# Softmax probabilities scaled in two steps, and latent norms behind each token tile's latent projection, in a two-layer hybrid-attention decoder

## The chip, the cores and the metric

The kernel runs on one core of one Trainium2 chip. The metric is the device time of one execution in microseconds (us). A core has a matrix engine (TensorE, PE in the rows, with PEld for its weight loads), a vector engine (VectorE, DVE), an activation engine (ScalarE, ACT), a general engine (GpSimd, POOL) and a queue engine that issues most of the transfers (SyncE, SP). Each engine executes its own list of instructions strictly in order, and waits on the others through semaphores.

## The reference

Two decoder layers over 512 tokens of width 1024, all in float32. Each layer has four groups of four attention heads, 64 wide, that share one input and one output projection, and then a SwiGLU network. The latent part of the third group (MLA), whose norms the change touches, and the attention that all groups end in are:

```python
h = rmsnorm(x, g_pre_mix[l])
z = jnp.einsum('bsd,de->bse', h, w_in[l])
z_moba, z_fox, z_fg, z_cq, z_ckv, z_kr, z_dil = jnp.split(z, SPLIT_POINTS, axis=-1)
...
c_q = rmsnorm(z_cq, g_mla_q[l])          # 192 wide
q_c = to_heads(jnp.einsum('bsr,re->bse', c_q, w_mla_q_up[l]), N_HEADS_MLA)
c_kv = rmsnorm(z_ckv, g_mla_kv[l])       # 128 wide
kv = to_heads(jnp.einsum('bsr,re->bse', c_kv, w_mla_kv_up[l]), N_HEADS_MLA)
...
sc = jnp.where(key_pos[None, :] <= q_pos[:, None], sc, -jnp.inf)   # every group: its own mask
p = jax.nn.softmax(sc, axis=-1)
return jnp.einsum('bhqk,bhkd->bhqd', p.astype(v.dtype), v)
...
x = x + rmsnorm(y, g_post_mix[l])        # y: output projection of the four groups
```

## The kernel before, in words

Tokens lie in four tiles of 128. Every float32 product is made of three matmuls on split operands (`mm3`: high by high, high by low, low by high), so each weight chunk is fetched into one of five `wraw` buffers by SyncE, copied to its high part by ScalarE (L168) and subtracted to its low part by VectorE (L173) or GpSimd (L171).

**A layer's first half (`mixing`).** The values of the first group (called fox) are projected, and token tile by token tile the latents: `ps_lat` (24 matmuls) is copied to `lat[t]` by ScalarE (L551). The fox queries follow (`ps_qk`, 24 matmuls for two heads). In a later loop over the token tiles the kernel before normalises the latents: ScalarE squares and sums (L595, L596), GpSimd makes the inverse root (L598 to L600), VectorE multiplies by it and by the gains `gqkv` (L601 for the 192 query columns, L602 for the 128 key-value columns); then TensorE turns the tile (transposes into `cq0T`, `cq1T`, `ckvT`, L604 to L606). The turned latents are split (`split`, L610 and L611, and `q1_stk`, L616 and L617), which is what the projections `ps_qup` and `ps_kvup` read.

**Attention (`attend`).** A unit is one head and a range of query tiles: four tiles (24 units: fox, MLA and MoBA heads in both layers) or two (16 units: the dilated heads). Per query tile TensorE makes scores `ps_s` (L454), VectorE adds the mask and finds the row's bound (`neg`, L457), and ScalarE takes the exponential with its row sum (L459, into `pr` and `den`). Query tile 0 has 128 keys, tile 3 has 512. After the last of them VectorE takes one reciprocal of all sums (L462), and GpSimd multiplies each tile of `pr` by it (L465). Then TensorE transposes blocks of 128x128 out of `pr` into `pT` (L474), ScalarE and VectorE split them (`turn`, L476 and L477), and TensorE applies them to the values (`weigh`, into `ps_o`, L482 and L483). The first turn of a four-tile unit takes the key tile 0 of all four query tiles. `weave` writes the units down so that the next unit's scores stand ahead of this unit's transposes, with projection matmuls of other groups in between; its two `pr` buffers allow that.

The order on each engine is that of the program as written, as a list scheduler rearranges it: it takes the instruction that stands earliest in the program among those that it estimates to be ready, and buffers of the pools (two `pr`, two banks for scores, two for transposes) hold it back. So moving a few lines also moves what stands around them, on every engine.

Of the kernel before, what the change touches and what calls it, by code (L numbers as in the profile page):

```python
# [9 lines left out]
F32 = mybir.dt.float32  # L10
F32R = mybir.dt.float32r
I32 = mybir.dt.int32
AF = mybir.ActivationFunctionType
ALU = mybir.AluOpType
PSUM = bass.MemoryType.PSUM

P = 128
# [6 lines left out]
EPS = 1e-6  # L24
# [13 lines left out]
L_CQ, L_CKV, L_KR = 4, 196, 324  # L38
# [43 lines left out]
def decoder(ctx, tc, x, positions, w_in, b_forget, g_mla_q, w_mla_q_up, g_mla_kv, w_mla_kv_up,  # L82
            w_out, g_pre_mix, g_post_mix, w_gate, w_up, w_down, g_pre_ffn, g_post_ffn, consts, out):
    nc = tc.nc
# [4 lines left out]
    small = ctx.enter_context(tc.tile_pool(name="small", bufs=8))  # L89
# [11 lines left out]
    def R(dt, name):  # L101
        return keep.tile([P, 512], dt, name=name, tag="ring", bufs=NR)

    def T(dt, name):
        return keep.tile([P, 512], dt, name=name, tag="temp", bufs=NTMP)
# [24 lines left out]
    mhalf = keep.tile([P, 2], F32, name="mhalf")  # L130
# [143 lines left out]
    def mixing(l, h_in, in_slots, out_slots, w_first):  # L274
# [163 lines left out]
        def attend(e0, tag, h, qa, qb, passes, vt, bias, more):  # L438
# [8 lines left out]
            for qt in range(qa, qb):  # L447
# [11 lines left out]
                nc.scalar.activation(p, p, AF.Exp, bias=neg[:, qt:qt + 1], scale=-1.0, accum_out=den[:, qt - qa:qt - qa + 1])  # L459
                offs[qt] = off  # L460
                off += nk
            nc.vector.reciprocal(den, den)  # L462
            for qt in range(qa, qb):
                p = pr[:, offs[qt]:offs[qt] + (qt + 1) * P]
                nc.gpsimd.tensor_scalar(p, p, den[:, qt - qa:qt - qa + 1], 1.0, op0=ALU.mult, op1=ALU.mult)  # L465
            yield
            ncol = (qb - qa) * P
            po = bank(ps_o, "ps_o")
# [63 lines left out]
        def window(col):  # L532
# [8 lines left out]
        lat_lo = [slot(s, F32R, "lat_lo") for s in out_slots[1:3]]  # L541
        wl = [weights(w_in[l, k * P:(k + 1) * P, C_LAT:C_LAT + N_LAT], [N_LAT],
                      into=(lat_hi[:, k, :], lat_lo[k // 4][:, k % 4, 0:N_LAT])) for k in range(KD)]
        for t in range(NT):
            for _ in steps[t][1]():
                pass
            ps = bank(ps_mm, "ps_lat")
            ts = slice(t * P, (t + 1) * P)
            for k in range(KD):
                mm3(ps[:, 0:N_LAT], hh(k, ts), hl(k, ts), *wl[k], k == 0, k == KD - 1)  # L550
            nc.scalar.copy(lat[t][:, 0:N_LAT], ps[:, 0:N_LAT])  # L551

        fox_passes, fox_qk = proj_qk(C_FOX, False)
        run(fox_qk[:1])
# [27 lines left out]
        if l == 0:  # L582
            with tc.issue_after(normed[0].ins), tc.issue_after(normed[1].ins):
                rope_tables()
        gains_lat = R(F32, "gqkv")
        gq, gkv = gains_lat[:, 0:192], gains_lat[:, 192:320]
        nc.sync.dma_start(gq, g_mla_q[l:l + 1, :].broadcast_to([P, 192]))
        nc.sync.dma_start(gkv, g_mla_kv[l:l + 1, :].broadcast_to([P, P]))
        jk = T(F32, "jk")
        pq0, pq1 = bank(ps_t, "cq0T"), bank(ps_t, "cq1T")  # L590
        pkv = bank(ps_s, "ckvT")
        for t in range(NT):
            ss = small.tile([P, 2], F32, name="ss2", tag="ss2")
            zq, zkv = lat[t][:, L_CQ:L_CKV], lat[t][:, L_CKV:L_KR]
            nc.scalar.activation(jk[:, 0:192], zq, AF.Square, accum_out=ss[:, 0:1])  # L595
            nc.scalar.activation(jk[:, 192:320], zkv, AF.Square, accum_out=ss[:, 1:2])  # L596
            r = small.tile([P, 2], F32, name="r2", tag="r2")
            nc.gpsimd.tensor_scalar(r[:, 0:1], ss[:, 0:1], 1.0 / 192, EPS, op0=ALU.mult, op1=ALU.add)  # L598
            nc.gpsimd.tensor_scalar(r[:, 1:2], ss[:, 1:2], 1.0 / 128, EPS, op0=ALU.mult, op1=ALU.add)
            nc.gpsimd.tensor_tensor(r, r, mhalf, op=ALU.pow)  # L600
            nc.vector.scalar_tensor_tensor(zq, zq, r[:, 0:1], gq, op0=ALU.mult, op1=ALU.mult)  # L601
            nc.vector.scalar_tensor_tensor(zkv, zkv, r[:, 1:2], gkv, op0=ALU.mult, op1=ALU.mult)  # L602
            ts = slice(t * P, (t + 1) * P)
            nc.tensor.transpose(pq0[:, ts], lat[t][:, L_CQ:L_CQ + P], ident)  # L604
            nc.tensor.transpose(pq1[0:64, ts], lat[t][:, L_CQ + P:L_CKV], ident)
            nc.tensor.transpose(pkv[:, ts], zkv, ident)  # L606
# [445 lines left out]
```

## Time and profile before

| what | value |
|---|---|
| time, median of 3 runs | 1266.09 us (1265.72 to 1267.85) |
| the profiled execution | 1268.2 us; span in the profile 1266.4 us |
| granted TensorE clock, mean | 0.996 of full speed |
| TensorE matmul busy | 1228.6 us, 97% of the span, 7044 matmuls |
| VectorE, ScalarE, GpSimd busy | 821.4 us (65%), 646.4 us (51%), 225.5 us (18%) |
| first halves of the two layers | about 14 to 265 us and 652 to 895 us of the span |

The span is what the profiler sees of the execution; 1.8 us of the time lie around it. A matmul's end is modelled in the records, so that matmuls that follow each other closely seem to overlap; the distance from start to start is what one takes.

### The profile page before, as it was taken

The page shows a single profiled execution, that of the slowest core. Times are in us where ns is not written, and L with a number is a line of the kernel's source. Part 1 is how long each engine was busy: PE and PEld are TensorE (multiplying, and loading weights), DVE is VectorE, ACT ScalarE, POOL GpSimd, SP SyncE. Part 2 cuts the span into 40 slices and gives each one's busy share as a digit, 9 for nine tenths or more (in the row PEclk, how much of TensorE's full clock was granted, in tenths as well). Part 3 has the DMA queues.
Part 4 walks back from the last instruction along what each step waited for, and adds up shares of the span by engine and source line. Part 5 has one row for each costly group of instructions (what it writes and reads, how often), then busy time and mean ns, then how long its engine had stood idle before and what let it go on. Part 6 is the DMA issues. An engine that isn't in the chain of part 4 may idle for free.

```text
span 1266.4 us, 19777 instructions
## 1 busy us (share of the span) xinstructions
PE 1228.6 (97%) x7044; PEld 1063.4 (84%) x7044; DVE 821.4 (65%) x1621; ACT 646.4 (51%) x1403; POOL 225.5 (18%) x305
## 2 busy tenths in 40 slices
PE   8999999999999999999999999999899999999998
PEld 7878877779989898888788788778798989898886
DVE  6876866787766666533466668676787666674334
ACT  6676756754434344422456767667553434353332
POOL 3223334443000000000131324433430000000001
PEclk9999999989999999999999999999999999999999
DMA  7221241521433333433342222324224333334331
GB/s 230 72 60 42 66 116 55 172 68 34 127 99 107 93 109 92 125 100 100 125 117 73 59 56 70 100 88 137 68 64 126 95 108 97 105 100 123 94 93 75
DMA packets 158054, 121.60 MB, mean 96 GB/s; under 512 B 9090, under 2 KB 133122, under 8 KB 157956
## 3 DMA queue, kind: packets, MB, share of 16 engines
q1 hardware_dynamic: 151908, 111.55, 30.3%
q10 hardware_dynamic: 6048, 8.80, 2.6%
q8 instruction: 55, 0.90, 0.3%
q14 instruction: 43, 0.35, 0.1%
HBM read 111.93 MB, written 4.19 MB: 92 GB/s over the span
## 4 chain that ended last, share of the span: by engine, by line
PE 75%; DVE 4%; ACT 2%; POOL 2%; issue 2%; DMA 1%; DVEq 0%; POOLq 0%; ACTq 0%; SPq 0%
PE ps_g L198 6%; PE ps_g L197 6%; PE ps_g L199 6%; PE ps_d L197 6%; PE ps_d L199 6%; PE ps_d L198 6%; PE ps L197 5%; PE ps L199 5%; PE ps L198 5%; PE ps_s L454 2%; PE ps_out L199 2%; PE pT L474 2%; PE ps_out L198 2%; PE ps_out L197 2%; PE ps_qk L197 2%; PE ps_qk L198 2%
## 5 line engine op out<-in xcount | busy, mean ns | idle before, releaser
L173 DVE TENSOR_TENSOR wlo<-wraw,whi 128x512 fp32r<-128x512 f32 x249 | 179.9, 729 | 149.7 <-ACT whi L168 144.8
L168 ACT CAST whi<-wraw 128x512 fp32r<-128x512 f32 x268 | 163.9, 620 | 213.2 <-PE ps_d L199 121.0
L198 PE MATMUL ps_g<-h,whi 128*128 128x512 f32 (+1 forms) x384 | 144.2, 376 | 5.0 <-DVE h L231 5.0
L197 PE MATMUL ps_g<-h,whi 128*128 128x512 f32 (+1 forms) x384 | 143.9, 375 | 1.4 <-ACT h L231 1.2
L199 PE MATMUL ps_g<-h,wlo 128*128 128x512 f32 (+1 forms) x384 | 143.6, 374 | 0.0
L876 ACT CAST whi<-wsum 128x512 fp32r<-128x512 f32 x80 | 49.7, 622 | 149.4 <-PE ps_g L198 71.9
L240 POOL TENSOR_SCALAR rstd<-ssp 128x1 f32<-128x1 f32 x16 | 6.9, 433 | 647.8 <-ACT jk L236 647.7
L465 POOL TENSOR_SCALAR pr<-pr,den 128x128 f32<-128x128 f32 (+3 forms) x128 | 78.1, 629 | 192.1 <-DVE den L462 188.6
L197 PE MATMUL ps_d<-whi,fh 128*128 128x512 f32 x288 | 112.2, 390 | 0.0
L199 PE MATMUL ps_d<-whi,fl 128*128 128x512 f32 x288 | 112.1, 389 | 0.0
L198 PE MATMUL ps_d<-wlo,fh 128*128 128x512 f32 x288 | 112.0, 389 | 0.0
L877 DVE TENSOR_TENSOR wlo<-wsum,whi 128x512 fp32r<-128x512 f32 x80 | 54.9, 690 | 83.0 <-ACT whi L876 83.0
L197 PE MATMUL ps<-sum,whi 128*128 128x256 f32 x320 | 90.2, 282 | 0.0
L198 PE MATMUL ps<-sum,whi 128*128 128x256 f32 x320 | 90.1, 282 | 0.0
L199 PE MATMUL ps<-sum,wlo 128*128 128x256 f32 x320 | 90.1, 281 | 0.0
L198 PEld LDWEIGHTS ps_g<-h,whi 128*128 128x128 f32 x384 | 73.1, 190 | 18.0 <-DVE h L231 6.2
L197 PEld LDWEIGHTS ps_g<-h,whi 128*128 128x128 f32 x384 | 73.1, 190 | 14.5 <-ACT h L231 2.7
L199 PEld LDWEIGHTS ps_g<-h,wlo 128*128 128x128 f32 x384 | 73.2, 191 | 12.6
L197 PE MATMUL ps_qk<-h,whi 128*128 128x512 f32 x192 | 76.8, 400 | 0.0
L199 PE MATMUL ps_qk<-h,wlo 128*128 128x512 f32 x192 | 75.7, 394 | 0.0
L198 PE MATMUL ps_qk<-h,whi 128*128 128x512 f32 x192 | 75.7, 394 | 0.0
L459 ACT ACTIVATE pr<-pr,neg 128x128 f32<-128x128 f32 (+3 forms) x128 | 71.5, 560 | 5.9 <-DVE neg L457 4.9
(312 smaller groups left out, 3335.2 us busy)
## 6 DMA issues: line engine op xcount, KB each, us to landing
wraw<-in_w_gate_dram SPq DMA_DIRECT2D x88, 256.0 KB, 3.4
wraw<-in_w_up_dram SPq DMA_DIRECT2D x88, 256.0 KB, 3.1
wraw<-in_w_down_dram SPq DMA_DIRECT2D x88, 256.0 KB, 2.8
wraw<-in_w_in_dram SPq DMA_DIRECT2D x72, 256.0 KB, 3.0
wraw<-in_w_out_dram SPq DMA_DIRECT2D x32, 256.0 KB, 2.9
xt<-in_x_dram SPq DMA_DIRECT2D x16, 256.0 KB, 4.4
rope_b<-rope_a ACTq DMA_DIRECT2D x64, 64.0 KB, 2.0
wraw<-in_w_in_dram SPq DMA_DIRECT2D x16, 178.0 KB, 3.6
```

The lines of the kernel that those rows point to most:

```text
L168: nc.scalar.copy(hi, raw)
L173: nc.vector.tensor_tensor(lo, raw, f32(hi), op=ALU.subtract)
L197: nc.tensor.matmul(ps, a_hi, b_hi, start=start, stop=False)
L198: nc.tensor.matmul(ps, a_hi, b_lo, start=False, stop=False)
L199: last_mm[0] = nc.tensor.matmul(ps, a_lo, b_hi, start=False, stop=stop)
L240: nc.gpsimd.tensor_scalar(r, ss[:, 0:1], ss[:, 1:2], EPS, op0=ALU.add, op1=ALU.add)
L454: nc.tensor.matmul(ps[:, 0:w], a if a.shape[-1] == P else a[:, qt * P:(qt + 1) * P], b[:, 0:w], start=i == 0, stop=i == n - 1)
L459: nc.scalar.activation(p, p, AF.Exp, bias=neg[:, qt:qt + 1], scale=-1.0, accum_out=den[:, qt - qa:qt - qa + 1])
L465: nc.gpsimd.tensor_scalar(p, p, den[:, qt - qa:qt - qa + 1], 1.0, op0=ALU.mult, op1=ALU.mult)
L474: nc.tensor.transpose(pt[:, i * P:(i + 1) * P], pr[:, offs[qt] + kt * P:offs[qt] + (kt + 1) * P], ident)
L876: nc.scalar.copy(hi, raw)
L877: nc.vector.tensor_tensor(lo, raw, f32(hi), op=ALU.subtract)
```

## The change

Two things. In `attend`, the reciprocal and the scaling of all query tiles but the last are written directly behind the last but one tile's exponential, as one reciprocal of three sums (of one sum in a two-tile unit) and a scaling per tile; the last tile has a reciprocal of its own and its scaling. The scalings are the same 128 in the whole program; there are 80 reciprocals instead of 40. In `mixing`, the squares, the inverse root and the two multiplications of a token tile's latents are written directly behind that tile's latent projection, and the transfers of their gains (`gqkv`) directly behind those of the latent weights. The matmuls are the same 7044.

```diff
                 nc.scalar.activation(p, p, AF.Exp, bias=neg[:, qt:qt + 1], scale=-1.0, accum_out=den[:, qt - qa:qt - qa + 1])
                 offs[qt] = off
                 off += nk
-            nc.vector.reciprocal(den, den)
-            for qt in range(qa, qb):
-                p = pr[:, offs[qt]:offs[qt] + (qt + 1) * P]
-                nc.gpsimd.tensor_scalar(p, p, den[:, qt - qa:qt - qa + 1], 1.0, op0=ALU.mult, op1=ALU.mult)
+
+                if qt >= qb - 2:
+                    new = range(qa, qt + 1) if qt == qb - 2 else [qt]
+                    d = den[:, new[0] - qa:qt - qa + 1]
+                    nc.vector.reciprocal(d, d)
+                    for t in new:
+                        p = pr[:, offs[t]:offs[t] + (t + 1) * P]
+                        nc.gpsimd.tensor_scalar(p, p, den[:, t - qa:t - qa + 1], 1.0, op0=ALU.mult, op1=ALU.mult)
             yield
...
                       into=(lat_hi[:, k, :], lat_lo[k // 4][:, k % 4, 0:N_LAT])) for k in range(KD)]
+        gains_lat = R(F32, "gqkv")
+        gq, gkv = gains_lat[:, 0:192], gains_lat[:, 192:320]
+        nc.sync.dma_start(gq, g_mla_q[l:l + 1, :].broadcast_to([P, 192]))
+        nc.sync.dma_start(gkv, g_mla_kv[l:l + 1, :].broadcast_to([P, P]))
+        jk = T(F32, "jk")
         for t in range(NT):
...
             nc.scalar.copy(lat[t][:, 0:N_LAT], ps[:, 0:N_LAT])
+            ss = small.tile([P, 2], F32, name="ss2", tag="ss2")
+            zq, zkv = lat[t][:, L_CQ:L_CKV], lat[t][:, L_CKV:L_KR]
+            nc.scalar.activation(jk[:, 0:192], zq, AF.Square, accum_out=ss[:, 0:1])
+            nc.scalar.activation(jk[:, 192:320], zkv, AF.Square, accum_out=ss[:, 1:2])
+            r = small.tile([P, 2], F32, name="r2", tag="r2")
+            nc.gpsimd.tensor_scalar(r[:, 0:1], ss[:, 0:1], 1.0 / 192, EPS, op0=ALU.mult, op1=ALU.add)
+            nc.gpsimd.tensor_scalar(r[:, 1:2], ss[:, 1:2], 1.0 / 128, EPS, op0=ALU.mult, op1=ALU.add)
+            nc.gpsimd.tensor_tensor(r, r, mhalf, op=ALU.pow)
+            nc.vector.scalar_tensor_tensor(zq, zq, r[:, 0:1], gq, op0=ALU.mult, op1=ALU.mult)
+            nc.vector.scalar_tensor_tensor(zkv, zkv, r[:, 1:2], gkv, op0=ALU.mult, op1=ALU.mult)
```

The same lines are gone from the later loop, which keeps its transposes.

What this does to the order of the engines is seen at three places. First TensorE at the latents of the first layer; it is the same in the second. `ps_qk` are the fox queries and, behind them, the fox keys; the three transposes per token tile write `cq0T`, `cq1T` and `ckvT`. Before, from the last matmuls of the keys on:

```order
L198 MATMUL ps_qk<-h,whi 128x512
L199 MATMUL ps_qk<-h,wlo 128x512
L604 MATMUL cq0T<-cst,lat 128x128
L605 MATMUL cq1T<-cst,lat 64x128
L604 MATMUL cq0T<-cst,lat 128x128
L605 MATMUL cq1T<-cst,lat 64x128
L606 MATMUL ckvT<-cst,lat 128x128
L197 MATMUL ps_qk<-h,whi 128x512
L606 MATMUL ckvT<-cst,lat 128x128
L198 MATMUL ps_qk<-h,whi 128x512
L604 MATMUL cq0T<-cst,lat 128x128
```

With the change, from the last matmuls of the queries on:

```order
L198 MATMUL ps_qk<-h,whi 128x512
L199 MATMUL ps_qk<-h,wlo 128x512
L609 MATMUL cq0T<-cst,lat 128x128
L610 MATMUL cq1T<-cst,lat 64x128
L611 MATMUL ckvT<-cst,lat 128x128
L609 MATMUL cq0T<-cst,lat 128x128
L610 MATMUL cq1T<-cst,lat 64x128
L611 MATMUL ckvT<-cst,lat 128x128
L609 MATMUL cq0T<-cst,lat 128x128
L610 MATMUL cq1T<-cst,lat 64x128
L611 MATMUL ckvT<-cst,lat 128x128
```

The twelve transposes stood behind 45 of the 48 `ps_qk` matmuls and among the last three; now they stand together behind the first 24, and the other 24 come between them and the first `ps_qup`.

Second, VectorE at the first MoBA head of the first layer (buffers numbered, since two units are in flight; `den` are this unit's sums, `v`, `wearly` and `wlo` other work, `mixf` the output of the unit before). Before:

```order
L457 ISA neg_1830 128x1
L477 TENSOR_TENSOR ptb1_96<-pT_1899,ptb0_95 128x384
L309 TENSOR_TENSOR v_889<-ps_v_1874,v_889 128x2x128
L173 TENSOR_TENSOR wearly_2270<-wraw_2276,wearly_2270 128x512
L462 RECIPROCAL den_1831<-den_1831 128x4
L173 TENSOR_TENSOR wlo_2053<-wraw_2051,whi_2052 128x512
L173 TENSOR_TENSOR wlo_2059<-wraw_2057,whi_2058 128x512
L173 TENSOR_TENSOR wlo_2116<-wraw_2114,whi_2115 128x512
L522 TENSOR_TENSOR mixf_1826<-ps_o_1858,mixt_1827 64x512
```

With the change:

```order
L457 ISA neg_1838 128x1
L481 TENSOR_TENSOR ptb1_96<-pT_1908,ptb0_95 128x384
L466 RECIPROCAL den_1839<-den_1839 128x3
L309 TENSOR_TENSOR v_889<-ps_v_1883,v_889 128x2x128
L173 TENSOR_TENSOR wearly_2282<-wraw_2288,wearly_2282 128x512
L466 RECIPROCAL den_1839<-den_1839 128x1
L173 TENSOR_TENSOR wlo_2063<-wraw_2061,whi_2062 128x512
L173 TENSOR_TENSOR wlo_2069<-wraw_2067,whi_2068 128x512
L457 ISA pr_1955,neg_1953<-ps_s_1956,cst_79 128x128
```

The reciprocal of three sums stands two instructions further ahead than the one of four stood, and that of the last sum stands in the old place.

Third, SyncE in the second layer, where the gains' two transfers lie among those of the weights (`128x356` are the latent weights, `x_mid` the first layer's output). Before:

```order
L167 DMA wraw<-in_w_in_dram 128x356 x4
L167 DMA wraw<-in_w_in_dram 128x4x128
L1020 DMA x_mid_78<-xt 128x512 x2
L167 DMA wraw<-in_w_in_dram 128x4x128 x3
L167 DMA wraw<-in_w_mla_q_up_dram 128x384
L182 DMA wraw<-in_w_mla_q_up_dram 64x384 x2
L167 DMA wraw<-in_w_mla_kv_up_dram 128x512
L167 DMA wraw<-in_w_in_dram 128x4x128 x4
L167 DMA wraw<-in_w_in_dram 128x2x256 x2
L587 DMA gqkv<-in_g_mla_q_dram 128x192
L588 DMA gqkv<-in_g_mla_kv_dram 128x128
L167 DMA wraw<-in_w_in_dram 128x2x256 x2
```

With the change:

```order
L167 DMA wraw<-in_w_in_dram 128x356 x4
L550 DMA gqkv<-in_g_mla_q_dram 128x192
L551 DMA gqkv<-in_g_mla_kv_dram 128x128
L167 DMA wraw<-in_w_in_dram 128x4x128
L1025 DMA x_mid_78<-xt 128x512 x2
```

The two transfers moved ahead of the 14 other weight transfers that stood in front of them. In the first layer they stand behind the third of the eight latent weight chunks.

## Rows read from the trace of the kernel before

**Rows 1.** The page: busy time of each engine with its share of the span and its instructions.

```profile
PE 1228.6 (97%) x7044; PEld 1063.4 (84%) x7044; DVE 821.4 (65%) x1621; ACT 646.4 (51%) x1403; POOL 225.5 (18%) x305
```

**Rows 2.** The waits of the whole span: engine, tile and line that waited, what released it; us in total, times, longest. PE are waits of the matmul stream, PEld those of the weight loads ahead of it.

```profile
PE pT L474 <- POOL pr L465: 7.2, 15, 0.9
...
PEld pT L474 <- POOL pr L465: 16.7, 35, 1.3
...
POOL pr L465 <- DVE den L462: 188.6, 29, 24.7
...
DVE den L462 <- ACT pr L459: 8.7, 14, 1.0
...
PE ps_lat L198 <- DVE lat_lo L173: 0.3, 1, 0.3
```

**Rows 3.** The timeline of the second layer's first fox head: start in us, duration, engine, line, instruction with how many of it in a row; in brackets the idle time ahead of it and what ended it.

```profile
700.26 0.72 ACT L459 ACTIVATE pr<-pr,neg 128x512 f32<-128x512 f32 x1
...
701.22 0.17 DVE L462 RECIPROCAL den<-den 128x4 f32<-128x4 f32 x1
...
701.49 3.18 POOL L465 TENSOR_SCALAR pr<-pr,den 128x128 f32<-128x128 f32 x4 [24.71 <-DVE den L462]
...
702.66 0.65 PE L474 MATMUL pT<-cst,pr 128*128 128x128 f32 x2
...
703.55 0.33 PE L474 MATMUL pT<-cst,pr 128*128 128x128 f32 x1 [0.24 <-POOL pr L465]
...
704.72 0.66 PE L474 MATMUL pT<-cst,pr 128*128 128x128 f32 x4 [0.84 <-POOL pr L465]
```

**Rows 4.** The timeline of the first layer's first MoBA head, from its last exponential to its first transposes, in the same columns.

```profile
154.31 0.71 ACT L459 ACTIVATE pr<-pr,neg 128x512 f32<-128x512 f32 x1
...
155.41 0.17 DVE L462 RECIPROCAL den<-den 128x4 f32<-128x4 f32 x1
155.65 1.99 DVE L173 TENSOR_TENSOR wlo<-wraw,whi 128x512 fp32r<-128x512 f32 x3
...
155.75 3.46 POOL L465 TENSOR_SCALAR pr<-pr,den 128x128 f32<-128x128 f32 x4 [8.92 <-DVE den L462]
...
157.16 0.33 PE L474 MATMUL pT<-cst,pr 128*128 128x128 f32 x1
...
159.27 0.66 PE L474 MATMUL pT<-cst,pr 128*128 128x128 f32 x4 [0.34 <-POOL pr L465]
```

**Rows 5.** TensorE's timeline at other units that stop: the third fox head, the third MoBA head (x5 in 1.42 us) and the first dilated head, all of the first layer.

```profile
95.32 0.66 PE L474 MATMUL pT<-cst,pr 128*128 128x128 f32 x4 [0.34 <-POOL pr L465]
...
191.52 1.42 PE L474 MATMUL pT<-cst,pr 128*128 128x128 f32 x5
...
210.39 0.55 PE L474 MATMUL pT<-cst,pr 128*128 128x128 f32 x3 [0.87 <-POOL pr L465]
```

**Rows 6.** Durations: four scalings in a row with no such instruction of VectorE beside them (timeline), and the reciprocals by form (busy us, mean ns of one, idle ahead of them).

```profile
122.84 2.06 POOL L465 TENSOR_SCALAR pr<-pr,den 128x128 f32<-128x128 f32 x4 [5.49 <-DVE den L462]
...
L462 DVE RECIPROCAL den<-den 128x4 f32<-128x4 f32 x24 | 4.2, 176 | 6.1 <-ACT pr L459 5.6
...
L462 DVE RECIPROCAL den<-den 128x2 f32<-128x2 f32 x16 | 2.6, 162 | 3.1 <-ACT pr L459 3.1
```

**Rows 7.** The latents: the multiplications by form, then the timeline of the second layer in order of time (GpSimd's last inverse root, the gains' first transfer, VectorE's first multiplications, TensorE's `ps_qk`, transposes, `ps_cum` and projections, the first splits).

```profile
L601 DVE SCALAR_TENSOR_TENSOR lat<-lat,r,gqkv 128x192 f32<-128x192 f32 x8 | 3.1, 411 | 2.5 <-DMA gqkv<-in_g_mla_q_dram 2.5
L602 DVE SCALAR_TENSOR_TENSOR lat<-lat,r,gqkv 128x128 f32<-128x128 f32 x8 | 2.6, 345 | 0.0
...
673.78 0.69 POOL L600 TENSOR_TENSOR r<-r,mhalf 128x2 f32<-128x2 f32 x1
...
679.20 0.46 SPq L587 DMA_DIRECT2D gqkv<-in_g_mla_q_dram  x1
...
681.70 0.39 PE L198 MATMUL ps_qk<-h,whi 128*128 128x512 f32 x1
681.93 0.39 PE L199 MATMUL ps_qk<-h,wlo 128*128 128x512 f32 x1
...
682.28 0.75 DVE L601 SCALAR_TENSOR_TENSOR lat<-lat,r,gqkv 128x192 f32<-128x192 f32 x2 [0.73 <-DMA gqkv<-in_g_mla_q_dram]
...
682.75 0.33 PE L604 MATMUL cq0T<-cst,lat 128*128 128x128 f32 x1 [0.44 <-DVE lat L601]
...
684.98 0.27 PE L606 MATMUL ckvT<-cst,lat 128*128 128x128 f32 x1
685.09 0.29 PE L679 MATMUL ps_cum<-fg,cst 128*128 128x16 f32 x2
...
685.90 0.42 PE L197 MATMUL ps_qup<-whi,sp_hi 128*128 128x384 f32 x1
...
686.17 0.68 DVE L611 TENSOR_TENSOR sp_lo<-cq0T,sp_hi 128x512 fp32r<-128x512 f32 x1
...
687.19 0.40 PE L198 MATMUL ps_kvup<-wlo,sp_hi 128*128 128x512 f32 x1
```

**Rows 8.** Windows of 2 us where a layer's first half hands over to its network, two of the first layer and one of the second: length, busy time of each engine with its instructions, then the granted TensorE clock, the DMA share and GB/s.

```profile
278.00:280.00 2.00, 1.27 (x6) 0.97 (x5) 2.00 (x3) 0.92 (x3) 0.43 (x1) 0.50 0.40 117
...
282.00:284.00 2.00, 2.00 (x11) 2.00 (x11) 2.00 (x4) 0.40 (x1) 0.00 (x0) 0.50 0.00 0
...
907.00:909.00 2.00, 2.00 (x17) 2.00 (x18) 1.35 (x3) 0.73 (x2) 0.86 (x2) 1.00 0.00 0
```

More of the change, by code (lines that the diff above doesn't have):

```diff
@@ L584, in mixing @@
                 rope_tables()
[L585 to L589, printed above, removed]
         pq0, pq1 = bank(ps_t, "cq0T"), bank(ps_t, "cq1T")
@@ L592, in mixing @@
         for t in range(NT):
[L593 to L602, printed above, removed]
+            zkv = lat[t][:, L_CKV:L_KR]
             ts = slice(t * P, (t + 1) * P)
```

## The prediction

> **What bounds the kernel now.** I read the page first: TensorE is busy 97% of the span [rows 1], so a change that leaves its 7044 matmuls as they are can only gain where TensorE stands still, and can only lose by making it stand still more. Next the table of waits, for what TensorE stands still for. In the layers' first halves the largest entry is the transposes' wait for GpSimd's scalings: 7.2 us in 15 stops of the matmul stream, and 16.7 us in 35 stops of the weight loads, part of which the matmul ahead covers [rows 2]. GpSimd in its turn waits for VectorE's reciprocal, and that for the exponentials, 8.7 us in 14 times (0.62 each) [rows 2]. Third, the timelines at those stops. In the second layer's first fox head the last exponential begins at 700.26 and takes 0.72; one reciprocal at 701.22; four scalings of 3.18 us together from 701.49; and TensorE, which came to the transposes at 702.66, gets the third block at 703.55 and the last four at 704.72 [rows 3]. The first three scalings needed nothing of the last exponential: that is the latency that the change attacks. The other stop is at the latents: the multiplication waits 0.73 us for gains that SyncE issued at 679.20, and the transposes wait for it [rows 7].
>
> What a stop costs is more than its gap. From 703.55 to 704.72 are 1.17 us; less the gap of 0.84 and one transpose of 0.11 (684.98 to 685.09 [rows 7]) 0.22 is left for starting up again [rows 3].
>
> **The scalings.** By starts minus 0.11 for each transpose, the units lose: first fox head 1.8 us (702.66 to 704.72 is 2.06, less three pitches of 0.11 is 1.73 [rows 3]); first MoBA head 2.0 (157.16 to 159.27 is 2.11, less 0.33 is 1.78, and the start-up of its last stop [rows 4]); third MoBA head 0.9 (five in 1.42 instead of 0.55 [rows 5]); first dilated head 1.1 (0.87 + 0.22); third fox head 0.6 (0.34 + 0.22) [rows 5]. With some 1.0 for the other dilated heads that is 7.4 us per layer, 14.8 in the two: between the 7.2 and the 16.7 of the two kinds of waits, as it must be, since 7.2 + 15 x 0.22 = 10.5 leaves out the stops that show only as stretched groups of transposes.
>
> What comes back is less. In the MoBA head the third exponential is over when the last begins, at 154.31, and the reciprocal now stands at 155.41 [rows 4]; with the change its first reciprocal stands two instructions further ahead on VectorE, right behind the exponential, so the scalings begin some 0.9 us earlier; in the fox head 1.0 (end of the third exponential near 700.3, against 701.22). The last tile's scaling takes its turn behind those three, so the last block is ready by about as much earlier, not by the whole wait. And the scheduler, which sees the scalings earlier, also moves transposes ahead: by the matmuls between a unit's last score and its transposes (0.11 to 0.23 each), the first fox head's first three stand 1.4 us earlier and its fourth 0.7, the third MoBA head's first 0.7, and the second layer's first halves nearly the same; only the first MoBA head's fourth stands 0.8 later, with the next unit's scores in the gap. So I leave waits of 1.2 us in each first fox head, 0.6 in each first and each third MoBA head, 0.6 in each first dilated head, 0.1 in each third fox head and 0.4 per layer in the rest: 3.5 per layer, 7.0 in all. **Gain 14.8 - 7.0 = 7.8 us.**
>
> Whether GpSimd can use its earlier start hangs on who works beside it. Four scalings take 2.06 us alone [rows 6], but 3.46 where three of VectorE's weight subtractions, each with two inputs in SBUF, run in the same stretch, and these take 1.99, 0.66 each [rows 4]. So GpSimd slows and VectorE doesn't. The earlier scalings meet the same subtractions and one more, at some 0.4 us for each; this is in the 0.6 left for the MoBA heads. The Trainium skill ("SBUF — State Buffer", section "Who interferes with whom") says that such a VectorE instruction and a GpSimd instruction that reads SBUF contend for one port pair, that whoever issues first holds it and the other blocks fully. By that rule an earlier GpSimd would hold VectorE up instead, up to a whole scaling at a time; the trace agrees that they contend but shows GpSimd paying (3.46 against 2.06).
>
> **The latents.** TensorE's last `ps_qk` ahead of the transposes starts at 681.93; with a pitch of 0.23 (681.70 to 681.93) its successor could start at 682.16, and starts at 682.75. From 681.93 to 685.09 stand four `ps_qk` and twelve transposes, 4 x 0.23 + 12 x 0.11 = 2.24; it takes 3.16, so 0.92 are lost. Then 685.90 to 687.19, three matmuls of some 0.18 and one of 0.23, 0.77, take 1.29: 0.52 lost to the splits [rows 7]. With 0.1 behind that it is 1.5 us, and by the same count 1.7 in the first layer. With the change the last token tile's inverse root is done at 673.78 + 0.69 = 674.47, and two multiplications of 0.41 and 0.35 make 675.2; the transposes stand 21 matmuls earlier, 682.16 - 21 x 0.23 = 677.3. So 2.1 us are spare. Behind them 24 matmuls of 0.23, 5.5 us, now lie ahead of the first `ps_qup`; the splits, three casts and three subtractions of 0.68 that partly overlap [rows 7], need some 4. **Gain 3.2 us**, and if VectorE should have a queue there, 1.6.
>
> The eight pairs of multiplications (3.1 + 2.6 us [rows 7]) are moved, not added; on the way they hold back the fox values' subtractions by 1 to 2 us, whose bank TensorE needs some 4 us later. SyncE's two gain transfers move past 14 weight transfers in the second layer, where SyncE stands waiting for a free `wraw` buffer (0.46 us to issue [rows 7]). In the first layer they go ahead of five latent weight chunks while the program starts, and TensorE already waits 0.3 there for the latent weights [rows 2]: nothing to 0.9 us, I take 0.2.
>
> **The forty new reciprocals.** No row shows one of three sums or of one; those of four and of two take 176 and 162 ns [rows 6], so 40 x 0.17 = 6.8 us on VectorE, at 65% busy. The cost to TensorE is at least nothing; at most the 6.8 plus a stop of 0.62 each where the queue waits for an exponential, 24.8. The three-sum reciprocal now waits for the third exponential where before the queue ran on, but its successors, mostly weight subtractions fetched well ahead, are rarely what TensorE waits for. I take a fifth of 6.8, 1.3. With the first layer's 0.2: **cost 1.5 us.**
>
> **Sum.** The profiled execution took 1268.2, span 1266.4 and 1.8 around it. 1268.2 - 7.8 - 3.2 + 1.5 = 1258.7. It was 2.1 above the median of the runs, so for the median 1266.1 - 9.5 = 1256.6: 1257.
>
> One thing not in the sum. At the first layer's hand-over the granted clock is 0.50 of full speed, the lower of its two levels (1.2 of 2.4 GHz), from 278 to 284, behind a stretch in which TensorE stood still for part of the time (1.27 of 2.00 us busy); in the second layer's it is 1.00 [rows 8]. Six us at half speed cost at most 3.0, and half of that, an estimate, since TensorE was not busy all the time. It may go, or come a second time: 1.5 us either way, in the range.
>
> **The rivals.** A difference of 0.2%, 2.5 us, is about the least that a measurement of this kernel tells from no change.
>
> Rival 1, the scalings come hardly earlier where it counts: port contention takes the 0.9 us back (a further 1.4 us, as between 2.06 and 3.46, would do it), and the transposes that now stand earlier run into the same wait. For it speak that both effects are in the rows and the order; against it that six of ten stopping units keep their place. Then 3.0 of the 7.8 remain: 1266.1 - 3.0 - 3.2 + 1.5 = 1261.4. Chance 0.20.
>
> Rival 2, no change: the scalings' waits turn into waits for the next in the chain (the splits of `pT`, the last tile's scaling), gain 0, and the latents give 1.6: 1266.1 - 1.6 + 1.5 = 1266.0. Against it speaks that each stop ends on GpSimd, with the splits well behind. Chance 0.10.
>
> Rival 3, slower: the new reciprocals stop VectorE's in-order queue, and the scores' masks and splits behind them come late. If every one of the 40 stops it for the 0.62 that the 14 stops had, and all reaches TensorE, it is 24.8 against the 11.0 gained: 1266.1 + 13.8 = 1279.9. It decides from 11.0 / 40 = 0.28 us per unit on, and shows from 0.34. For it: exponentials and reciprocals are only microseconds apart; against it: VectorE's 35% of idle time. The skill's rule on the port, if it held here against the row, would act at the same place and in the same direction. Chance 0.08.
>
> **How the numbers follow.** The forecast has 0.62, with a range of its own from 1250.5 (waits gone but for 3 us, nothing lost, clock pause gone: 14.8 - 3.0 + 3.2 = 15.0, near 1251) to 1260. To the range I add rival 1 with 2.5 us of its own: 1250.5 to 1264. Out of it are rivals 2 and 3. Faster by over 0.2% are the forecast and nearly all of rival 1, 0.80; the same 0.12; slower 0.08.
>
> **What would show it.** TensorE's waits for the scalings should fall from 7.2 and 16.7 us to about half; the first four scalings no longer one block of four; the waits for `lat` and the gains gone; 24 `ps_qk` between transposes and projections without a stop. I would be wrong if TensorE's waits for VectorE's `neg` or the `pT` splits grew by several us, if the scalings of a unit took well over 3.5 us, or if the first layer's start moved.

## The result, and the profile after

With the change the kernel takes 1255.63 us (median of 4 runs, 1255.0 to 1256.98) against 1266.97 us (4 runs) for the kernel before: a ratio of 0.9909 with a 95% interval of 0.9896 to 0.9922, or 11.3 us less. The prediction was 1257, which is 9.5 less than the 1266.1 that it started from, in a range of 1250.5 to 1264.

The page of the profiled execution (1255.16 us, span 1253.4) against [rows 1]: TensorE's share rises to 98%, VectorE has 40 instructions more.

```profile
PE 1222.2 (98%) x7044; PEld 1063.0 (85%) x7044; DVE 828.4 (66%) x1661; ACT 645.6 (52%) x1403; POOL 223.7 (18%) x305
```

The waits of the whole span, against [rows 2] (the lines of the scalings and reciprocals are now L469, L466, those of the transposes L478):

```profile
PE pT L478 <- POOL pr L469: 1.9, 7, 0.3
...
PEld pT L478 <- POOL pr L469: 9.6, 24, 0.7
...
POOL pr L469 <- DVE den L466: 151.8, 37, 22.3
...
DVE den L466 <- ACT pr L459: 6.0, 15, 0.5
...
PE ps_lat L198 <- DVE lat_lo L173: 0.3, 1, 0.3
```

The matmul stream's wait for the scalings fell from 7.2 to 1.9 us, the weight loads' from 16.7 to 9.6. TensorE's wait for the latents and VectorE's wait for the gains are gone from the list. The sign that the prediction named, half of both numbers, came for the weight loads and was passed by the matmul stream.

The first fox head of the second layer, against [rows 3]:

```profile
691.90 0.17 DVE L466 RECIPROCAL den<-den 128x3 f32<-128x3 f32 x1
692.16 0.73 ACT L459 ACTIVATE pr<-pr,neg 128x512 f32<-128x512 f32 x1
692.17 3.06 POOL L469 TENSOR_SCALAR pr<-pr,den 128x128 f32<-128x128 f32 x4 [22.29 <-DVE den L466]
...
693.16 0.79 PE L478 MATMUL pT<-cst,pr 128*128 128x128 f32 x2
...
694.18 0.33 PE L478 MATMUL pT<-cst,pr 128*128 128x128 f32 x1 [0.23 <-POOL pr L469]
...
695.28 0.66 PE L478 MATMUL pT<-cst,pr 128*128 128x128 f32 x4
```

The scalings begin with the last exponential (692.17 and 692.16); before they began 1.23 us behind its start. Still they run as one block of four, against the sign that the prediction named, since the last tile's reciprocal (693.12) is done before the third scaling is; the last four transposes start 0.05 us behind the block's end (695.23).

The first MoBA head of the first layer, against [rows 4]; two of the lines are the next unit's scores:

```profile
150.59 0.71 ACT L459 ACTIVATE pr<-pr,neg 128x512 f32<-128x512 f32 x1
150.77 0.17 DVE L466 RECIPROCAL den<-den 128x3 f32<-128x3 f32 x1
151.11 3.62 POOL L469 TENSOR_SCALAR pr<-pr,den 128x128 f32<-128x128 f32 x4 [8.00 <-PE ps_v L199]
151.16 0.68 DVE L173 TENSOR_TENSOR wearly<-wraw,wearly 128x512 fp32r<-128x512 f32 x1
...
153.29 0.58 PE L478 MATMUL pT<-cst,pr 128*128 128x128 f32 x2
...
154.11 0.33 PE L478 MATMUL pT<-cst,pr 128*128 128x128 f32 x1 [0.23 <-POOL pr L469]
...
154.45 0.34 PE L454 MATMUL ps_s<-klz,q_stk 128*128 128x384 f32 x1
...
154.86 0.40 PE L454 MATMUL ps_s<-klz,q_stk 128*128 128x512 f32 x1
155.09 0.60 PE L478 MATMUL pT<-cst,pr 128*128 128x128 f32 x4
```

From the last exponential's start to the first scaling it is 0.52 us instead of 1.44, and the four scores stand in what was the last wait.

The third fox head, the third MoBA head and the first dilated head of the first layer, against [rows 5]: the first runs its seven transposes at the pitch (six pitches of 0.11 and the last one's 0.27 make 0.93), the second still stops, the third has no gap in the matmul stream.

```profile
91.73 0.93 PE L478 MATMUL pT<-cst,pr 128*128 128x128 f32 x7
...
187.56 0.66 PE L478 MATMUL pT<-cst,pr 128*128 128x128 f32 x4 [0.34 <-POOL pr L469]
...
204.48 0.55 PE L478 MATMUL pT<-cst,pr 128*128 128x128 f32 x3
```

The latents of the second layer, against [rows 7]: the last inverse root, the last tile's first multiplication, the first and last of the twelve transposes, and the first split.

```profile
666.86 0.69 POOL L568 TENSOR_TENSOR r<-r,mhalf 128x2 f32<-128x2 f32 x1
...
667.59 0.42 DVE L569 SCALAR_TENSOR_TENSOR lat<-lat,r,gqkv 128x192 f32<-128x192 f32 x1 [0.68 <-POOL r L568]
...
670.48 0.27 PE L609 MATMUL cq0T<-cst,lat 128*128 128x128 f32 x1
...
671.68 0.27 PE L611 MATMUL ckvT<-cst,lat 128*128 128x128 f32 x1
...
674.62 0.69 DVE L616 TENSOR_TENSOR sp_lo<-cq0T,sp_hi 128x512 fp32r<-128x512 f32 x1
```

The twelve transposes run at their pitch (670.48 to 671.68 is 11 x 0.11). And the first layer's hand-over, against [rows 8]; the half clock now lasts from about 271.4 to 274.8, as worked out from the means of the windows, instead of from about 277.3 to 284.1, by the same working from means of 0.82 from 276 to 278 and 0.97 from 284 to 286:

```profile
270.00:272.00 2.00, 0.91 (x3) 0.71 (x4) 2.00 (x4) 1.12 (x4) 1.45 (x4) 0.86 0.12 34
272.00:274.00 2.00, 2.00 (x12) 2.00 (x10) 2.00 (x3) 0.20 (x1) 1.16 (x1) 0.50 0.80 239
274.00:276.00 2.00, 1.39 (x10) 1.09 (x10) 1.57 (x3) 1.54 (x5) 0.68 (x2) 0.79 0.00 0
```

**Where the time went.** I added up what every matmul's end comes later than its predecessor's by more than its own pitch (0.228 us for 512 columns, 0.172, 0.118 and 0.109 for 384, 256 and 128), over the whole execution. (This is a count of my own over all matmuls, not a view of the profile.) The sum is 70.2 us before and 57.2 after: 13.0 less, which is the difference of the two spans (1266.4 and 1253.4; the profiled execution of before lies above its median, so this is 1.7 more than the medians differ). By what was waited for: the scalings 14.7 and 7.4 us; the latents, their splits and the projections behind 4.9 and 0; matmuls stretched at the first hand-over without any wait 2.3 and 1.1; all else 0.5 more than before.

### The profile page after: what moved, and what is told of

Same layout as the page of the kernel before. It is cut to its first block, busy times and chain, and to the rows that moved or that the text cites. A ratio compares the mean times of both kernels' runs of the same rounds, so it can differ in the third digit from the quotient of the medians.

```text
span 1253.4 us, 19811 instructions
## 1 busy us (share of the span) xinstructions
PE 1222.2 (98%) x7044; PEld 1063.0 (85%) x7044; DVE 828.4 (66%) x1661; ACT 645.6 (52%) x1403; POOL 223.7 (18%) x305
## 4 chain that ended last, share of the span: by engine, by line
PE 82%; DVE 6%; ACT 4%; POOL 3%; issue 3%; DMA 2%; ACTq 0%; DVEq 0%; POOLq 0%
PE ps_g L198 6%; PE ps_g L197 6%; PE ps_g L199 6%; PE ps_d L197 6%; PE ps_d L199 6%; PE ps_d L198 6%; PE ps L197 5%; PE ps L199 5%; PE ps L198 5%; PE ps_s L454 3%; PE ps_qk L197 2%; PE ps_qk L198 2%; PE ps_qk L199 2%; PE pT L478 2%; POOL pr L469 2%
## 5 line engine op out<-in xcount | busy, mean ns | idle before, releaser
L173 DVE TENSOR_TENSOR wlo<-wraw,whi 128x512 fp32r<-128x512 f32 x249 | 182.5, 740 | 146.7 <-ACT whi L168 142.4
L469 POOL TENSOR_SCALAR pr<-pr,den 128x128 f32<-128x128 f32 (+3 forms) x128 | 75.7, 606 | 178.7 <-DVE den L466 151.8
```

What stands on the lines that cost most here:

```text
L173: nc.vector.tensor_tensor(lo, raw, f32(hi), op=ALU.subtract)
L469: nc.gpsimd.tensor_scalar(p, p, den[:, t - qa:t - qa + 1], 1.0, op0=ALU.mult, op1=ALU.mult)
```

## The experiments

Two theories stood against each other at first: that each half removes its own waits and pays alone, and that one of them does it all. Then it turned out that neither half needs its lines to be moved, which asked for what the cause was. All times are medians; the kernel before ran beside each of them (1267.0 to 1267.7 us). "Waits for the scalings" is the sum as above.

**Each half alone.** The scaling half is the first hunk of the diff, the norm half the rest of it.

> The scaling in two steps alone; the latent norms and their gains as before. Theory (each half pays for itself: the waits for the scalings 14.7 to about 7.4 us, the latent waits of 4.9 us stay): 6 to 8 us faster than the kernel before, the waits for the gains unchanged at 2.5 us. Rival (the gain comes from the latents' reordering and from the clock at the first layer's hand-over, the scalings only shift waits): 0 to 3 us faster.

Measured: 1262.37 us, ratio 0.9958 (0.9944 to 0.9971), 5.1 us faster; the waits for the scalings 8.7 us. VectorE's waits for the gains are there as before (2.8 us, 2.5 in [rows 7]). The gain lies between the two expectations: less than the 6 to 8 of the theory, more than the 3 of the rival.

```profile
PE pT L478 <- POOL pr L469: 4.0, 8, 1.0
DVE lat L605 <- DMA gqkv<-in_g_mla_q_dram: 2.8, 2, 1.8
```

> The latent norms behind each token tile and their gains early; one reciprocal and the scalings of a unit at its end, as before. Theory: the latent waits of 4.9 us fall to about 0, the waits for the scalings stay at 14.7: 3.5 to 5 us faster than the kernel before. Rival (the twelve transposes' wait comes back at the splits or the projections): 0 to 2 us faster.

Measured: 1262.99 us, ratio 0.9965 (0.9952 to 0.9977), 4.5 us faster; the waits for the scalings 13.7, those of the latents and projections 0.

```profile
PEld pT L474 <- POOL pr L465: 15.8, 34, 1.2
...
DVE lat L565 <- POOL r L564: 6.1, 6, 1.7
```

VectorE now waits for the inverse roots, one token tile at a time, 6.1 us in all; no matmul waits for that. Each half pays by itself. 5.1 + 4.5 = 9.6 is less than the 11.3 of both, though within the intervals; 1.3 us of the difference are in the waits for the scalings, 8.7 with the scaling half alone and 7.4 with both.

**The gains' transfers alone.** The four lines move, nothing else; the norms stay in the later loop.

```diff
+        gains_lat = R(F32, "gqkv")
+        gq, gkv = gains_lat[:, 0:192], gains_lat[:, 192:320]
+        nc.sync.dma_start(gq, g_mla_q[l:l + 1, :].broadcast_to([P, 192]))
+        nc.sync.dma_start(gkv, g_mla_kv[l:l + 1, :].broadcast_to([P, P]))
...
-        gains_lat = R(F32, "gqkv")
-        gq, gkv = gains_lat[:, 0:192], gains_lat[:, 192:320]
-        nc.sync.dma_start(gq, g_mla_q[l:l + 1, :].broadcast_to([P, 192]))
-        nc.sync.dma_start(gkv, g_mla_kv[l:l + 1, :].broadcast_to([P, P]))
```

> The kernel before with the two transfers of the gains moved behind the latent weights and nothing else: the norms are still written in the later loop. Theory (only the late gains held the norms; the place where the norms are written adds nothing, since the scheduler already ran the squares and inverse roots early and puts the transposes into the same place): the time of the norms-only kernel within 1 us, 3.5 to 5 us faster than before. Rival (the written place matters): less than half of the norms-only kernel's gain.

Measured: 1263.17 us, ratio 0.9966 (0.9953 to 0.9978), 4.3 us faster, the same as the whole norm half. The twelve transposes stand at the same place on TensorE, behind 24 `ps_qk`, and VectorE now waits for the inverse roots and no longer for the gains:

```profile
DVE lat L601 <- POOL r L600: 5.7, 5, 1.7
```

Moving the norms' lines brought nothing that can be told from noise; the late transfers were the cause. Whether it is their landing or the place that the scheduler then gives the transposes, no run separates: the one brings the other.

**Two reciprocals, at the end.** The kernel before, with the scalings left where they were written:

```diff
-            nc.vector.reciprocal(den, den)
+            nc.vector.reciprocal(den[:, 0:nq - 1], den[:, 0:nq - 1])
+            nc.vector.reciprocal(den[:, nq - 1:nq], den[:, nq - 1:nq])
```

> The kernel before with two reciprocals in place of one at a unit's end, of all sums but the last and of the last, the scalings behind both as before: the 40 new instructions without the earlier start. Theory (a reciprocal of 0.17 us on an engine with idle time): 0 to 2 us slower than before. Rival (the new instructions hold up the in-order queue): 3 to 7 us slower, the scalings' waits grow by that.

Measured: 1262.11 us, ratio 0.9953 (0.994 to 0.9966), 5.3 us faster: both expectations missed. The waits for the scalings are 8.0 us. I had meant it as the price of the instructions, but the first reciprocal does not depend on the last sum, so the scheduler puts it, and the first scalings, ahead by itself. It is the scaling half in another spelling.

**The price of forty reciprocals.** A reciprocal that nobody needs, behind the one of all sums, so that nothing can start earlier:

```diff
             nc.vector.reciprocal(den, den)
+            spare = small.tile([P, nq], F32, name="spare", tag="spare", bufs=2)
+            nc.vector.reciprocal(spare[:, 0:nq - 1], den[:, 0:nq - 1])
```

> The kernel before, with a further reciprocal per unit of the same size into a tile that nobody reads, behind the one of all sums: 40 more reciprocals and no earlier scaling. Theory (the price of the new instructions is small, and what the two-reciprocals kernel gained came from its first reciprocal no longer waiting for the last sum): 0 to 1.5 us slower than before, the waits for the scalings still 14 to 16 us. Rival (that kernel gained by a chance reordering): 2 to 5 us faster. Rival of the prediction (the queue is held up): 3 us or more slower.

Measured: 1264.67 us, ratio 0.9981 (0.9972 to 0.9991): 2.3 us faster, so neither my theory nor the held-up queue, but the rival of a reordering, at its small end. The waits for the scalings are 11.2 us instead of 14.7. In the order of TensorE's scores and transposes the extra instruction changed only the first MoBA head of each layer: its last four transposes now stand behind the next unit's scores, as with the change. That head in the first layer:

```profile
153.34 0.71 ACT L459 ACTIVATE pr<-pr,neg 128x512 f32<-128x512 f32 x1
...
154.44 0.17 DVE L462 RECIPROCAL den<-den 128x4 f32<-128x4 f32 x1
154.78 2.95 POOL L467 TENSOR_SCALAR pr<-pr,den 128x128 f32<-128x128 f32 x4 [8.91 <-DVE den L462]
...
157.12 0.33 PE L476 MATMUL pT<-cst,pr 128*128 128x128 f32 x1 [0.23 <-POOL pr L467]
...
158.10 0.60 PE L476 MATMUL pT<-cst,pr 128*128 128x128 f32 x4
```

The scalings begin 1.44 us behind the last exponential's start (153.34 to 154.78), exactly as before [rows 4], and the head loses 0.9 instead of 2.0 us. They also take 0.5 us less (2.95 against 3.46), since two of VectorE's subtractions run beside them and not three. Of the 1.1 us about 0.6 were the last stop, in whose place the scores now stand; the other 0.5 are smaller stops ahead of it. In the first fox heads, where no transpose moved, the loss went from 1.8 to 1.1: the scalings begin as late as before, 0.27 us behind the reciprocal, but take 2.48 us instead of 3.18 (3.18 in both layers before), and VectorE's second subtraction beside them takes 1.02 instead of 0.69. The first layer's fox head, with the last of its four scalings once more by itself:

```profile
70.78 0.72 ACT L459 ACTIVATE pr<-pr,neg 128x512 f32<-128x512 f32 x1
71.73 0.17 DVE L462 RECIPROCAL den<-den 128x4 f32<-128x4 f32 x1
72.00 2.48 POOL L467 TENSOR_SCALAR pr<-pr,den 128x128 f32<-128x128 f32 x4 [19.58 <-DVE den L462]
...
72.22 0.69 DVE L173 TENSOR_TENSOR wlo<-wraw,whi 128x512 fp32r<-128x512 f32 x1
...
73.80 0.69 POOL L467 TENSOR_SCALAR pr<-pr,den 128x512 f32<-128x512 f32 x1
...
74.00 1.02 DVE L173 TENSOR_TENSOR wlo<-wraw,whi 128x512 fp32r<-128x512 f32 x1
...
74.54 0.66 PE L476 MATMUL pT<-cst,pr 128*128 128x128 f32 x4 [0.34 <-POOL pr L467]
```

Before, the last scaling and the subtraction beside it in the same head:

```profile
74.00 1.20 POOL L465 TENSOR_SCALAR pr<-pr,den 128x512 f32<-128x512 f32 x1
...
74.03 0.69 DVE L173 TENSOR_TENSOR wlo<-wraw,whi 128x512 fp32r<-128x512 f32 x1
```

So 3.5 of the 7.3 us fewer waits come without any earlier scaling: from four scores in two heads, and from an accident in which engine waits for the other. What the forty instructions cost is not settled by this. In the profile TensorE's other stops, those at the half clock aside, sum to 0.2 us more than before; by the times 2.3 us (1.1 to 3.5) are gained where the waits fell by 3.5, so a cost between nothing and 2.4 us fits.

**The rest of the waits.** First every tile by itself, one reciprocal and scaling behind each exponential:

```diff
-                if qt >= qb - 2:
...
+                d = den[:, qt - qa:qt - qa + 1]
+                nc.vector.reciprocal(d, d)
+                nc.gpsimd.tensor_scalar(p, p, d, 1.0, op0=ALU.mult, op1=ALU.mult)
```

> The changed kernel with a reciprocal and a scaling for every query tile directly behind its own exponential (128 reciprocals of one sum). Theory (what is left of the waits, 7.4 us, is the last tile's turn behind the others, which an earlier first tile shortens a little, and each reciprocal costs little): 0 to 2 us faster than the changed kernel. Rival (VectorE's queue): 2 us or more slower than the changed kernel.

Measured: 1255.38 us, ratio 0.9909 (0.9895 to 0.9922), the same as the changed kernel; waits for the scalings 7.8. Earlier first tiles bring nothing more, and 48 more reciprocals (128 against 80) cost nothing that shows. Then the last tile away from GpSimd, to VectorE and to ScalarE:

```diff
-                        nc.gpsimd.tensor_scalar(p, p, den[:, t - qa:t - qa + 1], 1.0, op0=ALU.mult, op1=ALU.mult)
+                        (nc.vector if t == qb - 1 else nc.gpsimd).tensor_scalar(p, p, den[:, t - qa:t - qa + 1], 1.0, op0=ALU.mult, op1=ALU.mult)
```

> The changed kernel with the last tile's scaling on VectorE in place of GpSimd, so that it doesn't take its turn behind the others. Theory (the last tile's turn on GpSimd is the rest of the waits): the waits for the scalings fall from 7.4 to 2 to 4 us, 2 to 4 us faster than the changed kernel. Rival (VectorE's queue is the limit, 40 more instructions of 0.4 to 0.7 us on it): 0 to 4 us slower than the changed kernel, the waits for VectorE's neg and pT splits grow.

Measured: 1257.96 us, ratio 0.9928 (0.9915 to 0.994), 2.3 us slower than the changed kernel, at the edge of what the two intervals can tell apart. The waits for GpSimd's scalings did fall, to 4.4 us, but with 1.5 us of waits for VectorE's they are 5.9 of 7.4, and TensorE waits one step further on, at the values, where the splits of the transposes are late:

```profile
PEld pT L478 <- POOL pr L469: 4.9, 12, 0.8
...
PE ps_o L486 <- ACT pta L480: 2.9, 3, 1.8
PE ps_o L487 <- DVE ptb L481: 1.8, 2, 1.5
```

By the sum over all stops those at `ps_o` are 11.2 us, mostly for the splits, against 6.3 in the changed kernel.

```diff
-                        nc.gpsimd.tensor_scalar(p, p, den[:, t - qa:t - qa + 1], 1.0, op0=ALU.mult, op1=ALU.mult)
+                        if t == qb - 1:
+                            nc.scalar.mul(p, p, den[:, t - qa:t - qa + 1])
+                        else:
+                            nc.gpsimd.tensor_scalar(p, p, den[:, t - qa:t - qa + 1], 1.0, op0=ALU.mult, op1=ALU.mult)
```

> The changed kernel with the last tile's scaling on ScalarE, in place of GpSimd. Theory: as for VectorE, 2 to 4 us faster than the changed kernel, since ScalarE is idle for half of the span. Rival (the scaling waits in ScalarE's queue for the reciprocal, and the weight casts and the splits of the transposes wait behind it): 0 to 5 us slower than the changed kernel.

Measured: 1267.67 us, ratio 1.0004 (0.9994 to 1.0014): the whole gain of 11.3 us is gone, far more than the 0 to 5 of the rival. The waits for the scalings are the least of all, 3.8 us for GpSimd's and 0.5 for ScalarE's, but ScalarE's queue now stands for the last reciprocal, and VectorE waits longer for the exponentials:

```profile
DVE den L466 <- ACT pr L459: 12.5, 21, 1.2
...
PE ps_s L454 <- DVE neg L457: 2.9, 5, 0.9
PE ps_o L490 <- DVE ptb L484: 2.7, 2, 2.5
...
ACT pr L470 <- DVE den L466: 2.6, 7, 0.6
```

By the sum over all stops the scores are not where most of it is lost (1.3 us more than in the changed kernel): the stops at `ps_o` grew by 9.0 us, 7.6 of them for the splits of the transposes on ScalarE and VectorE, and those at the transposes ahead of the networks (`hnT`) by 3.7, mostly at the two hand-overs; 2.4 us more are half clock in this one profile. What makes those splits late was not followed further.

So the 7.4 us that are left are not to be had by giving the last scaling to one of these two engines.

**The two causes and no moved line.** The gains' transfers early, and the two reciprocals at the end; together the two diffs above.

> The kernel before with only the two things that paid so far: the gains' transfers moved behind the latent weights, and two reciprocals (of all sums but the last, and of the last) in place of one, at the unit's end as written; no scaling and no norm is written earlier. The transposes stand at the same places among TensorE's matmuls as with the whole change. Theory (the scheduler places the lines itself; what counts is that the first tiles' scaling no longer depends on the last sum and that the gains are there): within 1.5 us of the changed kernel, 10 to 12 us faster than before. Rival (the written place of the scalings and norms matters): 3 us or more slower than the changed kernel.

Measured: 1254.77 us, ratio 0.9898 (0.9884 to 0.9913), the waits for the scalings 7.4: the changed kernel's result, with nothing moved but two transfers.

**GpSimd's subtractions.** One constant, `SHARE_HEADS` from 10 to 0, takes GpSimd's weight subtractions during the attention to VectorE. By the trace they are nine, not eight: GpSimd's of 128x512 go from 22 to 13.

> The changed kernel with all weight subtractions during the attention on VectorE: the eight that GpSimd did there are taken off it. Theory (VectorE's subtractions and GpSimd's instructions that read SBUF hold each other up): VectorE's longest subtractions in the attention, 1.5 to 1.8 us beside GpSimd's, fall to 0.7, and the time is 0 to 2 us less than the changed kernel's. Rival (VectorE's queue has no room for eight more of 0.7 us): 1 to 5 us slower than the changed kernel.

Measured: 1256.59 us, ratio 0.9906 (0.9889 to 0.9923), no different from the changed kernel. VectorE's subtractions of over 0.8 us are 23, in place of 24: the long ones beside GpSimd's subtractions in the attention are gone, others beside its rotary products (`rope_b`) came in their place. What GpSimd's subtractions cost there can't be told from nothing by this run.

## Why the prediction was right, point by point

**The bound was TensorE's standing still.** Right: the matmuls are the same, and the time that their stops lost accounts for all 13.0 us between the spans.

**The scalings.** Forecast 14.8 us of waits now, 7.0 left; measured 14.7 and 7.4. By units of the first layer, forecast and measured: first fox head 1.2 and 1.3, third fox head 0.1 and 0, first MoBA head 0.6 and 0.65, third MoBA head 0.6 and 0.7, first dilated head 0.6 and 0.3, the rest 0.4 and 0.7; the last two misses cancel. So the count by starts and pitches, and the discount for transposes that the scheduler moves ahead, hold. What I had not sized is where the gain comes from. I gave the MoBA head 0.9 us for the earlier start and let the scores in the gap help; the spare reciprocal shows that with scalings as late as before, but with the scores in the gap and scalings 0.5 us shorter, 1.1 of that head's 1.35 come. The first fox heads lose 1.1 with the spare reciprocal and 1.3 with the change, so there, where the change also takes four transposes earlier, the earlier start brought nothing that the accident did not. The earlier start is what cures the third fox head, where no matmul moved (0.7 to 0, and 0.7 still with the spare reciprocal), and the first dilated heads (1.1 to 0.3, and 1.0 still).

**The forty reciprocals.** A fifth of 6.8, 1.3 us, was the term. It was probably too much, but that is argued: the spare reciprocals leave room for 0 to 2.4 us, and the 48 further ones behind each exponential left the time as it was (1255.38 and 1255.63). VectorE is idle for a third of the span, and its waits for the exponentials, which the new instructions might have lengthened, fell from 8.7 us [rows 2] to 6.0.

**The latents.** Forecast 3.2 us, measured 4.3 to 4.5. The mechanism is the forecast one: the last tile was ready at 668.3 (667.59 and two multiplications), 2.2 us ahead of the transposes, for a forecast 2.1. The transposes' part was right, 2.0 us in the two layers. The projections' part was short: 0.6 us a layer forecast, 1.2 measured, because I put 0.1 for everything behind 687.19, and there a `ps_qup` waits for the third of the splits (0.5 us a layer); the scores' wait for `klz` (0.2 a layer) went as well.

**The first layer's start.** 0.2 us were set aside for two more transfers ahead of the latent weights; the wait there is 0.3 us before and after, so nothing.

**The clock.** Left out of the sum and put at 1.5 us either way. It came on the good side: the stretch at 0.50 got shorter, and the stretched matmuls there fell by 1.3 us. The window that the prediction took for the cause, TensorE busy 1.27 of 2.00 us from 278 on, lies inside the stretch, which began at about 277.3; ahead of it TensorE was busy 1.10 of 2.00 us from 274 to 276. All that is in this one execution: at the hand-overs of the other profiled executions the matmuls stretched at 0.50 sum to between 0 (the two causes and no moved line) and 3.9 us (the gains' transfers alone), without an order that fits what was changed. So it blurs a comparison of two profiles by as much. The times are medians of executions whose mean granted clocks spread alike, 0.995 to 0.999 before and 0.996 to 0.999 with the change.

**The sum.** -7.8 - 3.2 + 1.5 = -9.5 forecast; the halves measured -5.1 and -4.5, both together -11.3. With its reciprocals the scaling half was forecast at -7.8 + 1.3 = -6.5, the latents with the first layer's start at -3.2 + 0.2 = -3.0: 1.4 too much and 1.5 too little. That the forecast met the halves' sum of -9.6 so closely is luck. That the whole lies in the range rests on the mechanisms: the latents' is as forecast, the scalings' in part, since 3.5 of their 7.3 us come without an earlier start too.

**The rivals.** Transposes taken earlier did run into the same wait in the first fox heads (1.3 left of 1.8) and in the third MoBA heads (0.7 left of 0.9), but the other units came free; that rival was worth its place, not its 1261. The held-up queue and the waits turning into others did not happen with the change. They did when the last scaling went to VectorE or ScalarE.

**Where I read too much from one row.** I took from the MoBA head that GpSimd slows and VectorE doesn't. That holds in that head. Elsewhere it is the other way, as the changed kernel's rows show:

```profile
155.94 1.29 POOL L534 TENSOR_TENSOR mix<-mixf,mix 128x512 fp32r<-128x512 f32 x1 [1.21 <-ACT mix L533]
156.26 1.53 DVE L173 TENSOR_TENSOR wlo<-wraw,whi 128x512 fp32r<-128x512 f32 x1
```

A subtraction that takes 0.68 alone takes 1.53 when GpSimd began 0.3 us ahead of it. There are 24 such of over 0.8 us in the changed kernel and 19 in the one before. The Trainium skill ("SBUF — State Buffer", section "Who interferes with whom") says that whichever starts first holds the shared ports; the trace agrees here and seems not to in the first MoBA head, where a subtraction that began 0.05 us behind the scalings took its usual 0.68 and GpSimd paid (3.62 against 2.06). The fox head's last scaling shows both outcomes: before, a subtraction that began 0.03 us behind the scaling took its 0.69 and the scaling 1.20; with the spare reciprocal one that began 0.20 us behind took 1.02 and the scaling 0.69. Each time one of the two waited and the other did not. Which one, the recorded starts don't tell at distances as small as 0.05 us; GpSimd's times in a profile are rough, so these rows don't refute the rule. It does reach TensorE at times: with the spare reciprocals, in the fox heads, the scalings took 0.7 us less and TensorE's loss was 0.7 less.

## What to carry to other kernels

Look for the dependency, not the place in the source: with a list scheduler a line written late is placed early as soon as its inputs allow it, so what paid were one reciprocal cut in two, so that three tiles no longer wait for the fourth, and two transfers issued ahead of others. Count stops of the bounding engine by starts and pitches, unit by unit, and allow for the scheduler spending part of an earlier result on starting its consumer earlier. And price a reordering before explaining a small gain: an instruction that does nothing moved this kernel by 2.3 us.

## What the hardware showed that was not expected

Putting one scaling per unit on ScalarE, an engine busy half of the time, in place of GpSimd cost 12 us, the whole gain: an engine's free time did not tell what a waiting instruction in its queue would cost. And which of two engines waited for the other changed with a shift of 0.1 to 0.2 us between them, worth 0.7 us of TensorE's time in a head.
